# Gate chunks before a branch projection, later transposes, split first loads, and identity products at the start of a hybrid decoder layer

## The chip, the cores and the metric

The kernel runs on one core of a Trainium2 chip. The metric is the device time of one execution, in microseconds (us), as the median of the runs shown. A profiled execution gives the trace; its span runs from the first to the last instruction. Engines are named as in the profile: PE (TensorE, matrix products) with PEld (its weight loads), DVE (VectorE), ACT (ScalarE), POOL (GpSimd) and SP (SyncE, which here only issues DMAs).

## The reference, cut to what matters

One decoder layer with 256 tokens and 2048 channels, all in float32:

```
h  = rms_norm(x, norm_mix)
qa,ka,va, u, qc,kc,vc, gates = split(h @ w_in)       # 3*1024, 1024, 3*1024, 3*2048 columns
ya = block_attention(qa,ka,va)                       # "a": softmax with a relative bias
yb = multiscale_pool(u)                              # "b"
yc = stick_breaking_attention(qc,kc,vc)              # "c"
g  = sigmoid(gates)                                  # three gates of 2048 channels
m  = g[0]*(ya @ w_br_a) + g[1]*(yb @ w_br_b) + g[2]*(yc @ w_br_c)
x1 = x + m @ w_out
x2 = x1 + swiglu(rms_norm(x1, norm_ffn))             # 5632 hidden channels
out = rms_norm(x2, norm_final)
```

## The kernel before, in words

**Products.** Every float32 operand of a large product is split into two parts, hi (rounded) and lo (the rest), and a product is three: hi by hi, lo by hi, hi by lo. `split` (L105 to L112) does it: ACT writes hi (L108, with a scale L111), DVE subtracts to get lo (L109, L112). Splitting a piece of a weight matrix is called cutting it here. Output columns are worked in chunks of 512 (CH), rows of a weight matrix in units.

**Groups and units.** The work is a list of groups (L1008 to L1022), each one chunk of output columns, and each group is a list of units. A unit is fetched (DMA by SP), cut (ACT, DVE) and multiplied (PE). A projection of 2048 rows with two row tiles a unit has 8 units; `br`, a branch projection of 1024 rows, has 4 units for branch a (span 2) and 2 units for b and c (span 4). `gate(n, 0, ...)` has 8 units. `gate_pair` works two chunks at once by a form of Strassen's scheme (class `Squares`): seven PSUM banks collect the partial products, and its units come in three kinds, N (24 products), Wp (9) and Ws (12), in the order N Wp Ws N Wp Ws N Wp Ws Wp Ws N.

**Order.** `run` (L475) goes through the units. Before unit j is multiplied, the units up to j+3 are cut (two ahead in the first six units), as far as a bound on slots allows; `ahead` issues the fetches. DVE, ACT, PE and SP each execute their own instructions in the order in which they are written out, so a unit's cut stands behind all that was written out earlier on DVE and ACT. In the first eight units, the cut is preceded by `prepare_x`, which transposes two column tiles of x on PE and splits them; that of unit 1 is written out before unit 0 is multiplied.

**Work beside.** `beside(gen, after, lag)` puts a generator on a list; `step_side` advances one generator after each unit: the first on the list that is due, `after` units after it was put there, then every `lag` units. The end of a generator takes a step of its own. An advanced generator goes to the end of the list. `finish_side` (L269) advances until the list is empty, with no units between.

- Stick-breaking attention (branch c): `all_stick`, four pairs of heads; each pair takes five units of steps: scores (L667, L669) and exponentials (L674 to L677); sums (L679, L680) and masks; split; a step left out, then triangular products (L689 to L691) and exponentials (L692); values (L583, L584) with the next pair's scores. It starts two units after the last group of qkv c.
- `br(0, 0)` calls `finish_side` ahead of its first unit, then `open_late`, which replaces a pool of buffers, and then puts `add_differences` on the list (eight steps, every second unit), whose results `gate_pair` needs.
- The merged sums m, after branch c: `turn()` of `br(n, 2)` transposes 4 tiles of 128 columns in two steps. `transposed` (L234) takes a PSUM bank, two transposes on PE (L238), hi on ACT, lo on DVE; the bank is free when lo is written. For n = 0 and 1 these steps fall into the following `gate_pair(1, 2)`.

**Buffers.** `slots` has 22 tiles of 8 KB a partition for weights, x and intermediate results; `wk` has 8 tiles of 128 by 512; PSUM has 8 banks.

**Start and end.** SP issues mix_rows, both x tiles (128 tokens by 512 columns each), and the first weights as four parts of 256 KB, then further x columns and weights. PE's first instruction is `columns(0, mix_rows)`. At the end each half of the tokens is normalised, scaled by DVE (n = 0, 3) and ACT (n = 1, 2), and written by four DMAs on SP (L1000 to L1006). The first half's writing goes on while PE works on the second half.

The order of the groups around the change:

```
groups += qkv("c", 4 * WIDTH, start_stick)
groups += [gate(n, 0, True) for n in range(2)] + [br(n, 0, True) for n in range(2)]
for n in range(2, D_MODEL // CH):
    groups += [gate(n, 0, False), br(n, 0)]
```

With the third argument True, `gate` writes its scaled sums without the sigmoid, and `br` applies it (L845), so that ACT keeps the tables of the exponentials while stick attention runs.

Of the kernel before, what the change touches and what calls it, by code (L numbers as in the profile page):

```python
# [16 lines left out]
P = 128  # L17
D_MODEL = 2048
SEQ = 256
# [13 lines left out]
CH = 512  # L33
# [18 lines left out]
def trunk(ctx: ExitStack, tc: tile.TileContext, x, norm_mix, norm_ffn, w_in, w_pool, pool_scale,  # L52
# [49 lines left out]
    def toks(t):  # L102
        return slice(t * P, (t + 1) * P)
# [85 lines left out]
    def load_x(c):  # L189
        for t in range(NT):  # L190
            nc.sync.dma_start(xt[t][:, cols(c)], x[toks(t), cols(c)])

    mix_rows = const.tile([KT, P], F32, name="mix_rows")
    nc.sync.dma_start(mix_rows, norm_mix[0].rearrange("(k p) -> k p", p=P))
    load_x(0)
    nrows = const.tile([KT + HEADS, P], F32, name="nrows")
    rel = const.tile([HEADS, REL_BUCKETS], F32, name="rel")

# [4 lines left out]
    def columns(c, rows):  # L203
        k = rows.shape[0]
        pt = bank()
        nc.tensor.transpose(pt[:, :k], rows, ident[:k, :k])
        nc.vector.tensor_copy(ncols[:, c:c + k], pt[:, :k])

    columns(0, mix_rows)

    def load_rows():
# [35 lines left out]
    def prepare_x(kt):  # L247
        transposed(xT(kt), [xt[t][:, kt * P:(kt + 1) * P] for t in range(NT)], ncols[:, kt:kt + 1])
# [5 lines left out]
    def beside(gen, after=2, lag=2):  # L254
        side.append([clock[0] + after, lag, gen])
# [219 lines left out]
    def run(units, startup):  # L475
        loads = [u for _, u in units if u.loads]
        done = {"fetch": 0, "cut": 0}

        def fetch():
            k = done["fetch"]  # L480
            if k in (1, 2, 3):
                load_x(k)
            if k == 4:
                load_rows()
            if k == 0:
                loads[k].fetch(parts=4)
            else:
                loads[k].fetch()
            done["fetch"] += 1

        def ahead(n):
            while done["fetch"] < min(n, len(loads)):
                fetch()

        opened = 0
        j = 0
        while j < len(units):
            lead = 2 if j < KT // 2 - 2 else 4
            if j == 0:
                ahead(2)  # L500
            while done["cut"] < min(j + lead, len(units)):
                u = done["cut"]
                g, unit = units[u]
                if u >= KT // 2 and sum(v.need for _, v in units[j:u]) + unit.need > cap[0]:
                    break
                if j:
                    ahead(opened + 3 if u > 7 else opened + 2)
                if u < KT // 2:
                    prepare_x(2 * u)
                    prepare_x(2 * u + 1)  # L510
                    unit.cut(step=None if u else 1)
                else:
                    unit.cut()
                done["cut"] += 1
                opened = sum(v.loads for _, v in units[:u + 2]) - 1 if u + 1 < len(units) else opened + 1
            if j:
                ahead(opened + 3 if done["cut"] > 7 else opened + 2)
            g, unit = units[j]
            if unit.first and g.before:
                g.before()  # L520
            if g.staggered and len(units) - j == 2:
                for p in range(len(g.parts)):
                    for k in range(2):
                        units[j + k][1].multiply([p])
                    g.after(g.acc[p], *g.parts[p])
                return
            unit.multiply()
            if j in startup:
                startup[j]()
            if unit.last:  # L530
                g.after(g.acc if isinstance(g, Group) else g.banks)
            clock[0] += 1
            step_side()
            j += 1
# [282 lines left out]
    def br(n, b, plain=False):  # L817
# [21 lines left out]
        def after(acc):  # L839
            if b == 2 and n == 0:  # L840
                mT.append(Halves())
            for t in range(NT):
                g = gates[n][t]
                if plain:
                    nc.scalar.activation(g, g, AF.Sigmoid)  # L845
                if b == 0:
                    nc.vector.tensor_mul(m[n][t], acc[t], g)
                else:
                    nc.vector.tensor_mul(g, acc[t], g)
                    nc.vector.tensor_add(m[n][t], m[n][t], g)  # L850
            if b == 2:
                beside(turn(), lag=1)

        return Group(lhs, range(HEADS), w_br[b], 0, n * CH, after, before, span=4 if b else 2)

# [128 lines left out]
    def final_norm(acc, t, c):  # L984
# [15 lines left out]
        for n in (0, 1, 3, 2):  # L1000
            hn = h[t][:, cols(n)]
            if n in (0, 3):
                nc.vector.tensor_scalar(hn, hn, a[9], None, OP.mult)
            else:
                nc.scalar.activation(hn, hn, AF.Copy, scale=a[9])
            nc.sync.dma_start(out[toks(t), cols(n)], hn)  # L1006

    groups = qkv("a", 0, start_block)  # L1008
    groups += [channels("u", 3 * WIDTH, c, start_pooling if c else None) for c in range(2)]
    groups += qkv("c", 4 * WIDTH, start_stick)  # L1010
    groups += [gate(n, 0, True) for n in range(2)] + [br(n, 0, True) for n in range(2)]
    for n in range(2, D_MODEL // CH):
        groups += [gate(n, 0, False), br(n, 0)]
    for b in range(1, 3):
        for i in range(2):
            groups += [gate_pair(i, b), br(2 * i, b), br(2 * i + 1, b)]
# [48 lines left out]
```

## Time and profile before

| | us |
|---|---|
| median of 3 runs | 1577.0 (1576.76 to 1577.03) |
| the profiled execution | 1576.42 |
| its span | 1574.7 |
| PE busy | 1545.7 (98%) |
| DVE busy | 1094.3 (69%) |
| ACT busy | 745.9 (47%) |
| mean granted clock of PE, share of full speed | 0.994 |

The first table of the profile gives the busy time of each engine. A line of the trace in time order gives the start, the length, the engine, the line of the program and the operation, what is written from what, and in brackets how long the engine sat idle before and what ended that. A row of merged instructions (x4) gives their common length. PE's products overlap: one starts before the one ahead of it has ended, so the step from start to start is its cost.

### The profile page before, as it was taken

The numbers are of one execution on the slowest core, as the hardware profiler recorded it, in microseconds if no ns is written. First come the engines' busy times: TensorE is split into PE (matmuls) and PEld (weight loads), VectorE is DVE, ScalarE is ACT, GpSimd is POOL, SyncE is SP. The second block draws the span as 40 slices with busy tenths as digits, with TensorE's granted clock in tenths as the row PEclk, the third lists the DMA queues.
The fourth block names the chain that finished last, engine by engine and source line by source line (L and its number), as shares of the span: only waits on it lengthen the run. The fifth ranks groups of instructions, "written<-read, shape, count | busy, mean of one in ns | idle before, by whom it ended". The sixth has DMA issues, their size and how long they took to land.

```text
span 1574.7 us, 19128 instructions
## 1 busy us (share of the span) xinstructions
PE 1545.7 (98%) x7873; PEld 1322.6 (84%) x7873; DVE 1094.3 (69%) x1064; ACT 745.9 (47%) x724; POOL 25.6 (2%) x94
## 2 busy tenths in 40 slices
PE   8999999999799999999999999999999999999997
PEld 8998999988688888877888878888888888888886
DVE  6453665644486988978556888667886668867685
ACT  7423443446454545635455555434454435543363
POOL 2000000101000000000000000000000000000000
PEclk9999999999899999999999999999999999999999
DMA  9654455553355745647555655556665556655661
GB/s 344 219 188 161 142 186 174 168 187 134 116 179 200 249 151 205 242 148 257 188 190 174 214 187 204 197 162 212 212 213 190 165 185 212 226 191 172 208 219 54
DMA packets 144167, 300.12 MB, mean 191 GB/s; under 512 B 6432, under 2 KB 7504, under 8 KB 143952
## 3 DMA queue, kind: packets, MB, share of 16 engines
q1 hardware_dynamic: 143776, 297.84, 55.7%
q8 instruction: 61, 1.00, 0.3%
q0 software_dynamic: 304, 1.06, 0.2%
q14 instruction: 26, 0.21, 0.0%
HBM read 296.77 MB, written 2.11 MB: 190 GB/s over the span
## 4 chain that ended last, share of the span: by engine, by line
PE 96%; DVE 2%; ACT 1%; issue 0%; DMA 0%; POOL 0%; SPq 0%; ACTq 0%; DVEq 0%; POOLq 0%
PE bank L440 37%; PE bank L333 13%; PE bank L334 13%; PE bank L338 13%; PE bank L353 5%; PE bank L355 5%; PE bank L361 5%; DVE slot L109 1%; PE bank L938 1%; ACT slot L108 1%; PE bank L583 1%; PE bank L238 0%; DMA slot<-in_x_dram 0%; PE bank L584 0%; DVE slot L422 0%
## 5 line engine op out<-in xcount | busy, mean ns | idle before, releaser
L109 DVE TENSOR_TENSOR slot<-slot,slot 128x2048 fp32r<-128x2048 f32 (+3 forms) x406 | 719.3, 1799 | 191.0 <-ACT slot L108 190.0
L108 ACT ACTIVATE slot<-slot 128x2048 fp32r<-128x2048 f32 (+3 forms) x406 | 601.5, 1517 | 346.6 <-DVE slot L424 136.8
L440 PE MATMUL bank<-slot,slot 128*128 128x512 f32 x1719 | 440.4, 391 | 0.0
L440 PEld LDWEIGHTS bank<-slot,slot 128*128 128x128 f32 x1719 | 322.7, 188 | 66.8
L333 PE MATMUL bank<-slot,slot 128*128 128x512 f32 (+1 forms) x936 | 365.0, 390 | 0.0
L334 PE MATMUL bank<-slot,slot 128*128 128x512 f32 (+1 forms) x936 | 362.8, 388 | 0.0
L440 PE MATMUL bank<-slot,late 128*128 128x512 f32 x1014 | 279.1, 390 | 0.0
L338 PE MATMUL bank<-slot,slot 128*128 128x512 f32 (+1 forms) x936 | 236.5, 387 | 0.0
L440 PEld LDWEIGHTS bank<-slot,late 128*128 128x128 f32 x1014 | 189.7, 188 | 39.2 <-DVE slot L109 0.2
L333 PEld LDWEIGHTS bank<-slot,slot 128*128 128x128 f32 x936 | 176.4, 188 | 35.4
L334 PEld LDWEIGHTS bank<-slot,slot 128*128 128x128 f32 x936 | 176.3, 188 | 35.3
L338 PEld LDWEIGHTS bank<-slot,slot 128*128 128x128 f32 x936 | 174.9, 188 | 35.9
L353 PE MATMUL bank<-slot,slot 128*128 128x256 f32 x640 | 159.6, 287 | 0.2 <-ACT slot L108 0.2
L355 PE MATMUL bank<-slot,slot 128*128 128x256 f32 x640 | 157.7, 284 | 0.0
L353 PEld LDWEIGHTS bank<-slot,slot 128*128 128x128 f32 x640 | 123.5, 193 | 0.7 <-ACT slot L108 0.6
L355 PEld LDWEIGHTS bank<-slot,slot 128*128 128x128 f32 x640 | 123.5, 193 | 0.0
L361 PE MATMUL bank<-slot,slot 128*128 128x256 f32 x640 | 89.8, 283 | 0.0
L108 ACT ACTIVATE slot<-bank 128x512 fp32r<-128x512 f32 (+1 forms) x46 | 23.2, 520 | 127.6 <-PE bank L938 67.7
L361 PEld LDWEIGHTS bank<-slot,slot 128*128 128x128 f32 x640 | 82.6, 192 | 0.0
L109 DVE TENSOR_TENSOR slot<-bank,slot 128x512 fp32r<-128x512 f32 (+1 forms) x46 | 26.8, 596 | 56.6 <-ACT slot L108 56.6
L422 DVE TENSOR_TENSOR slot<-slot 128x1024 f32<-128x1024 f32 x49 | 59.7, 1219 | 0.0
L973 DVE TENSOR_TENSOR slot<-bank,slot 128x512 f32<-128x512 f32 x30 | 19.6, 686 | 55.5 <-PE bank L338 55.5
(158 smaller groups left out, 626.1 us busy)
## 6 DMA issues: line engine op xcount, KB each, us to landing
slot<-in_w_in_dram SPq DMA_DIRECT2D x103, 1024.0 KB, 5.0
slot<-in_w_gate_dram SPq DMA_DIRECT2D x88, 512.0 KB, 3.9
slot<-in_w_up_dram SPq DMA_DIRECT2D x88, 512.0 KB, 4.9
slot<-in_w_down_dram SPq DMA_DIRECT2D x44, 1024.0 KB, 5.2
slot<-in_w_out_dram SPq DMA_DIRECT2D x16, 1024.0 KB, 5.6
slot<-in_w_br_a_dram SPq DMA_DIRECT2D x8, 1024.0 KB, 5.1
slot<-in_w_br_b_dram SPq DMA_DIRECT2D x8, 1024.0 KB, 5.4
slot<-in_w_br_c_dram SPq DMA_DIRECT2D x8, 1024.0 KB, 5.1
```

What stands on the lines that cost most here:

```text
L108: nc.scalar.activation(hi, src, AF.Copy)
L109: nc.vector.tensor_tensor(lo, src, f32(hi), OP.subtract)
L333: nc.tensor.matmul(acc[:, c], hi[:, toks(t)], whi[:, j, c], start=i + j == 0, stop=False)
L334: nc.tensor.matmul(acc[:, c], lo[:, toks(t)], whi[:, j, c], start=False, stop=False)
L338: nc.tensor.matmul(acc[:, c], hi[:, toks(t)], wlo[:, j, c], start=False, stop=i + j == n - 1)
L353: nc.tensor.matmul(o, whi[:, j, w], hi, start=i + j == 0 and c % 2 == 0, stop=False, skip_group_check=True)
L355: nc.tensor.matmul(o, whi[:, j, w], lo, start=False, stop=False, skip_group_check=True)
L361: nc.tensor.matmul(o, wlo[:, j, w], hi, start=False, stop=i + j == n - 1 and c % 2 == 1, skip_group_check=True)
L422: nc.vector.tensor_tensor(s[:, 0:2], raw[:, 0:1].to_broadcast([P, 2, CH]), raw[:, 1:3], OP.add)
L440: nc.tensor.matmul(g.banks[b], x, w[:, k, :], start=start, stop=g.left[b] == 0)
L583: nc.tensor.matmul(py[:, i, :], v[:, 0, s], pA[i], start=True, stop=False)
L973: nc.vector.tensor_add(h[t][:, cs], acc[t], h[t][:, cs])
```

## The change

- Group order: gate chunks 0, 1, 2, then `br` 0, 1, 2 of branch a (all with the sigmoid in `br`), then gate chunk 3 and `br` 3. Before it was gate 0, 1, br 0, 1, gate 2, br 2, gate 3, br 3.
- `turn()` of `br(0, 2)` and `br(1, 2)` becomes due 4 units after it is listed, not 2.
- The first x load is split: columns 0 to 255 of tokens 0 to 127 on SP, those of tokens 128 to 255 on ACT's queue, then mix_rows and columns 256 to 511 of both on ACT's queue. mix_rows and `load_x(0)` leave SP.
- `warm_up(n)` multiplies the identity by itself n times into a PSUM bank that nothing reads: 8 times ahead of `columns(0, ...)`, and 3 times after the transposes of unit 0.
- In the final writing, the DMAs of n = 1 and 2 are issued by ACT.

```diff
@@ -191,8 +191,12 @@
     mix_rows = const.tile([KT, P], F32, name="mix_rows")
-    nc.sync.dma_start(mix_rows, norm_mix[0].rearrange("(k p) -> k p", p=P))
-    load_x(0)
+    first, rest = slice(0, SEQ), slice(SEQ, CH)
+    nc.sync.dma_start(xt[0][:, first], x[toks(0), first])
+    nc.scalar.dma_start(xt[1][:, first], x[toks(1), first])
+    nc.scalar.dma_start(mix_rows, norm_mix[0].rearrange("(k p) -> k p", p=P))
+    for t in range(NT):
+        nc.scalar.dma_start(xt[t][:, rest], x[toks(t), rest])
@@ -206,6 +210,13 @@
+    def warm_up(n):
+
+        o = bank()
+        for _ in range(n):
+            nc.tensor.matmul(o[:, :P], ident, ident, start=True, stop=True)
+
+    warm_up(8)
     columns(0, mix_rows)
@@ -508,6 +519,8 @@
                     prepare_x(2 * u)
                     prepare_x(2 * u + 1)
+                    if u == 0:
+                        warm_up(3)
                     unit.cut(step=None if u else 1)
@@ -849,7 +862,7 @@
             if b == 2:
-                beside(turn(), lag=1)
+                beside(turn(), after=4 if n < 2 else 2, lag=1)
@@ -1003,14 +1016,13 @@
-            nc.sync.dma_start(out[toks(t), cols(n)], hn)
+            (nc.sync if n in (0, 3) else nc.scalar).dma_start(out[toks(t), cols(n)], hn)
-    groups += [gate(n, 0, True) for n in range(2)] + [br(n, 0, True) for n in range(2)]
-    for n in range(2, D_MODEL // CH):
-        groups += [gate(n, 0, False), br(n, 0)]
+    groups += [gate(n, 0, True) for n in range(3)] + [br(n, 0, True) for n in range(3)]
+    groups += [gate(3, 0, False), br(3, 0)]
```

## Rows read from the trace of the kernel before

**Rows 1.** The page's first table: busy time of each engine, its share of the span, and its instructions.

```profile
PE 1545.7 (98%) x7873; PEld 1322.6 (84%) x7873; DVE 1094.3 (69%) x1064; ACT 745.9 (47%) x724; POOL 25.6 (2%) x94
```

**Rows 2.** PE's waits over the whole span: what waited for what, us in total, how often, the longest.

```profile
PE bank L689 <- ACT t L108: 7.1, 1, 7.1
PE bank L238 <- DVE slot L109: 5.2, 1, 5.2
PE bank L238 <- DMA slot<-in_x_dram: 3.4, 2, 2.3
```

**Rows 3.** Busy time in stretches of 20 us: the stretch, its length, then PE, PEld, DVE, ACT and POOL with their instructions, the granted clock of PE as a share of full speed, the DMA share and GB/s.

```profile
400.00:420.00 20.00, 11.99 (x47) 9.83 (x46) 5.73 (x7) 10.26 (x17) 2.30 (x6) 0.76 0.32 106
...
700.00:720.00 20.00, 14.79 (x66) 11.93 (x65) 14.42 (x16) 9.20 (x11) 0.00 (x0) 0.91 0.32 106
```

**Rows 4.** PE in order of time, from the triangular products of the third pair of heads to the values of the fourth.

```profile
398.78 0.39 PE L689 MATMUL bank<-t,tri 128*128 128x512 f32 x1
...
399.71 0.40 PE L333 MATMUL bank<-slot,slot 128*128 128x512 f32 x1
...
402.46 0.59 PE L583 MATMUL bank<-t,slot 128*128 128x256 f32 x2
...
403.76 0.60 PE L667 MATMUL bank<-slot,slot 128*128 128x256 f32 x2
...
404.85 0.38 PE L669 MATMUL bank<-slot,slot 128*128 128x128 f32 x2
412.30 0.79 PE L689 MATMUL bank<-t,tri 128*128 128x512 f32 x1 [7.07 <-ACT t L108]
...
415.46 1.22 PE L583 MATMUL bank<-t,slot 128*128 128x256 f32 x2 [0.95 <-POOL t L656]
416.48 0.63 PE L584 MATMUL bank<-t,slot 128*128 128x128 f32 x2
```

**Rows 5.** PE in order of time, the first unit of `br(0, 0)`: its first product, and the four products that end it.

```profile
418.04 0.77 PE L333 MATMUL bank<-slot,slot 128*128 128x512 f32 x1
...
421.13 1.07 PE L338 MATMUL bank<-slot,slot 128*128 128x512 f32 x4
```

**Rows 6.** DVE in order of time: the gated products after `br(1, 0)`, then the first instruction (L174) of three successive steps of `add_differences`; between these stand the rest of the step and the lo parts of two cuts.

```profile
442.09 1.28 DVE L847 TENSOR_TENSOR slot<-bank,wk 128x512 f32<-128x512 f32 x2
443.29 0.69 DVE L174 TENSOR_TENSOR wk<-slot 128x512 f32<-128x512 f32 x1
...
448.14 0.69 DVE L174 TENSOR_TENSOR wk<-slot 128x512 f32<-128x512 f32 x1
...
453.86 0.69 DVE L174 TENSOR_TENSOR wk<-slot 128x512 f32<-128x512 f32 x1
```

**Rows 7.** All engines in order of time at the begin of `gate_pair(1, 2)`: every row of PE that transposes m for n = 0 and 1 (L238), and the rows of DVE and PE around the wait.

```profile
694.05 0.60 PE L238 MATMUL bank<-ident,slot 128*128 128x128 f32 x4
...
699.99 0.60 PE L238 MATMUL bank<-ident,slot 128*128 128x128 f32 x4
...
702.49 0.60 PE L238 MATMUL bank<-ident,slot 128*128 128x128 f32 x4
...
704.00 1.22 DVE L422 TENSOR_TENSOR slot<-slot 128x1024 f32<-128x1024 f32 x1
...
705.74 0.38 PE L238 MATMUL bank<-ident,slot 128*128 128x128 f32 x2
...
710.85 0.42 DVE L109 TENSOR_TENSOR slot<-bank,slot 128x256 fp32r<-128x256 f32 x1
...
711.33 0.69 PE L238 MATMUL bank<-ident,slot 128*128 128x128 f32 x2 [5.21 <-DVE slot L109]
...
711.66 4.13 PE L440 MATMUL bank<-slot,slot 128*128 128x512 f32 x12
...
712.47 0.43 DVE L109 TENSOR_TENSOR slot<-bank,slot 128x256 fp32r<-128x256 f32 x1 [1.20 <-ACT slot L108]
```

**Rows 8.** All engines in order of time at the start: PE's transposes of x for units 0 and 1, the first and the last products of unit 0, and the transposes for unit 2.

```profile
6.63 1.76 PE L238 MATMUL bank<-ident,slot 128*128 128x128 f32 x7 [1.17 <-DMA slot<-in_x_dram]
...
8.62 0.58 PE L353 MATMUL bank<-slot,slot 128*128 128x256 f32 x1 [0.23 <-ACT slot L108]
...
11.66 1.12 PE L361 MATMUL bank<-slot,slot 128*128 128x256 f32 x8
...
12.62 0.60 PE L238 MATMUL bank<-ident,slot 128*128 128x128 f32 x4
```

**Rows 9.** The chain that ended last, in order of time, at the start: start, length, what.

```profile
1.72 4.87 DMA slot<-in_x_dram
```

**Rows 10.** All engines in order of time at the end: the scaling of the first half of the tokens and what follows it on ACT and DVE, and the last four issues of the output on SP.

```profile
1563.48 1.34 ACT L1005 ACTIVATE slot<-slot,st 128x512 f32<-128x512 f32 x2 [1.21 <-DVE st L999]
...
1564.73 0.42 ACT L989 ACTIVATE wk<-slot 128x256 f32<-128x256 f32 x1
...
1566.24 0.42 DVE L988 TENSOR_TENSOR slot<-bank,slot 128x256 f32<-128x256 f32 x1 [0.47 <-PE bank L338]
...
1569.05 1.80 SPq L1006 DMA_DIRECT2D out_dram<-slot  x4
```

**Rows 11.** DMA issues of two short stretches (2.1 to 2.6 us, the first part of the first weights; 4.05 to 5.1 us, the second x columns): what is loaded, how often, KB each, us from issue to landing.

```profile
slot<-in_w_in_dram SPq DMA_DIRECT2D x1, 256.0 KB, 5.1
...
slot<-in_x_dram SPq DMA_DIRECT2D x2, 256.0 KB, 6.0
```

## The prediction

> **What bounds the kernel now.** I read the table of busy times first: PE is busy 98% of the span, DVE 69%, ACT 47% [rows 1]. So only what lets PE idle, or slows its clock, can give time back, and what DVE and ACT do more counts only where PE comes to wait for it. Next the list of PE's waits [rows 2]. Three stand out: 7.1 us once for the hi part of a stick-attention tile, 5.2 us once for a transpose (L238) that waits for a DVE instruction, and 3.4 us for the first x loads. The table of stretches then shows what a wait costs beside itself: around 400 us PE is busy 12.0 of 20 us and its mean granted clock is 0.76, around 700 us 14.8 of 20 us and 0.91 [rows 3]; elsewhere the lower of its two levels (1.2 and 2.4 GHz) hardly shows. The reader is to see that four places are in play (start, 405, 705 and the end) and that each long wait is followed by some microseconds at half clock. The lines in order of time at those places price the parts.
>
> **Part 1, three gate chunks ahead of branch a.** Stick attention starts two units after qkv c, takes five units for a pair of heads and four pairs, so its last step falls in the 22nd unit. Before, two gate chunks give 16 units; the rest of the fourth pair is worked off in `finish_side` with no units between, and PE waits there. With three chunks there are 24 units, so the list is empty when `br(0, 0)` begins. What that is worth: PE's last score products start at 404.85, so the next could start near 405.05; the first product of `br(0, 0)` starts at 418.04. Between lie products that take 0.93 us (398.78 to 399.71) and 1.30 us (402.46 to 403.76) when the same step of the third pair stands among units [rows 4, 5]. Lost: 418.04 - 405.05 - 2.23 = 10.8 us. After it the first eight products take 3.09 us (418.04 to 421.13); the four that follow start (1.07 - 0.40)/3 = 0.22 us apart, so eight cost 1.8 at full clock: 1.3 us more [rows 4, 5]. Sum **-12.1**. The cover is the eight units of gate chunk 2, some 22 us; the wait list has the triangular products waiting once only, so those of the three pairs that stood among units were hidden [rows 2].
>
> What becomes late next: three branch groups in a row, with `add_differences` beside them. DVE needs 4.85 us for a step of kind N with two cuts (443.29 to 448.14), 5.72 for one of kind W (448.14 to 453.86), and 1.28 for the gated products after each group [rows 6]. Twelve units of 12 products at 0.22 to 0.23 are 32.5 us of PE; six steps (three of each kind) and three sets of gated products are 31.7 + 3.8 = 35.5 us of DVE. It falls 3 us behind, but cuts are written out three units (8 us) ahead, and eight gate units follow with little else on DVE. I take 0, with 0 to +3 as bounds. The gate sums that now wait in six of the eight `wk` tiles leave two for a step, which is what one step uses.
>
> **Part 2, transposes of m later.** Count units from the end of `br(1, 2)`, and call the first unit of `gate_pair(1, 2)` u0. Before, the four steps stand after `br(1, 2)`, u0, u1 and u2, at 694.05, 699.99, 702.49 and 705.74 [rows 7]. Each transposes two tiles, and each tile needs a PSUM bank. After u2 (N, Wp and Ws done) seven banks hold partial products and one is left. So the second tile of that step waits until the first one's lo part is written, and DVE does that at 710.85, behind the sums and lo parts of two cuts that it began at 704.00: this is the wait of 5.21 us [rows 7]. Now the change. With `after=4` the first chunk's steps fall after u0 and u1. The second chunk's first step falls after u2, a generator's end takes the turn after u3, and its second step falls after u4. **A step after u2 is still there**, behind the same cuts and with one free bank, so I expect the 5.2 us to stay. The step after u4 is new, with one free bank as well; no cut is written out between u3's and it, so DVE is free, and the second tile waits only for the first one's hi and lo: from the begin of a transpose to the end of lo took 711.33 to 712.90, 1.6 us, here at the lower clock; less its own 0.3, some 1.2 us [rows 7]. The step that leaves 694.05 had no wait. Sum **+1.2**; below, 0; above, +6.5, if the new step meets DVE as busy as the old one (5.2 and the slow products after it).
>
> **Part 3, the start.** PE's transposes of x now go on at 6.63, when the second x load has landed (4.87 us after 1.72); unit 0's first product starts at 8.62, after hi parts and the first cut [rows 8, 9]. Unit 0's first 16 products take 3.04 us (8.62 to 11.66); its last eight take 1.12 together, 0.12 apart, so 16 cost 1.9 at full clock [rows 8]. *The clock:* 11 identity products (two instructions each) keep PE at work beforehand. A pair of instructions with 256 columns took 1.02 us at the lower clock (415.46 to 416.48), so one with 128 some 0.5, and eight some 4 us [rows 4]. Begun when the identity is written, near 2 us (an estimate), they end near 6, before x is complete, so they cost nothing and I count the 1.1 us in full (0 if the clock doesn't rise). *The loads:* unit 1's transposes are written out ahead of unit 0's products and need columns 256 to 511, so the last x load decides again. It is now the fourth issue on ACT, and issues cost 1.80/4 = 0.45 us each [rows 10], so it goes out about as late as now, but unit 0's hi parts and first cut no longer stand behind it: what follows is four transposes, 0.6 us [rows 8], in place of 2.0. The first weights go out two issues earlier, 0.9 us, and took 5.1 us [rows 11]: they land near 6.4, and the cut adds 0.6. So the first product starts between 7.0 and 7.8; I take 7.5, **-1.1**. The next cover is thin: the second x columns, issued near 4.1 and 4.6, take 6.0 us and are needed for the transposes at 12.62 [rows 8, 11]; with 0.9 us earlier issue they land at 9.2 to 9.7, for a need near 10.4. Both together **-2.2**, bounds 0 and -3.2. ACT's four issues take 1.8 us, ahead of its table load and constants, all before its first hi part near 6.
>
> Here a rule speaks against the change. The row says that the second x load, 256 KB, took 4.87 us after its issue [rows 9]. The Trainium skill ("DMA: Bandwidth & Descriptors", section "Issuing engines are not separate DMA queues") says that all queues end on the same 16 DMA engines, so that a second one saves only the time of issuing. By that the loads give one issue, 0.45, in place of 1.1, and the total would be 0.6 us higher.
>
> **Part 4, the end.** ACT scales two chunks in 1.34 us [rows 10]. If an issue holds ACT as it holds SP, 0.45 us each, the two of the first half push the square at 1564.73 back by 0.9; DVE had 0.47 us of idle before 1566.24 [rows 10], so the last chain starts 0.4 later. At the very end SP's four issues take 1.80 us after DVE's first scaling, which is half of that pair's time; ACT's two scalings and two issues in turn take 0.67 + 0.45 + 0.67 + 0.45 = 2.2, the same end. Sum **+0.4**. If an issue costs ACT nothing, the last one goes out some 0.5 us earlier: -0.5. No row shows an issue on ACT; I take the upper end, since SP's rows are the nearest.
>
> The Trainium skill ("Perfetto Trace Analysis", section "DMA Instruction — HWDGE (DVE, Sync)") says that the issuing sequencer is free only when the descriptors are generated. By that the end costs the 0.4; without it the total would be 0.9 lower.
>
> **Sum.** -12.1 + 1.2 - 2.2 + 0.4 = -12.7 on the profiled execution's 1576.4, so 1563.7; the median is 0.6 above that execution: 1564.3 us.
>
> **Rivals.** (a) *The wait at 705 goes too.* For it: a bank or DVE could be free earlier with the first step moved from 694 on. Against: the three steps after u0, u1, u2 keep their places. Then 5.2, the slow products after it (12 take 4.13 against 12 x 0.225 = 2.7, so 1.3 [rows 7]) and the new 1.2 are gained: 1556.6. Chance 0.16. (b) *DVE falls behind in the branch groups*, or the new step after u4 meets a busy DVE: +3 to +5, 1567 to 1569. For it: the 35.5 against 32.5 us above. Chance 0.13. (c) *Slower than before:* the steps of `add_differences` come into PE's way whole, because slots or `wk` tiles shorten the lead of the cuts to nothing. A step is 2.4 (N) or 3.3 us (W) of DVE without its cuts of 2.4 [rows 6]; six of them are 17 us, so 1581. It decides from 2.1 us of PE wait a step (12.7/6) on. Against it: the lead of three units, and no such wait in the list with the same steps [rows 2]. Chance 0.03. (d) *The change doesn't do what it says:* the list isn't empty at `br(0, 0)`, and the wait stays: 1564.3 + 12.1 = 1576. Chance 0.04.
>
> **How the numbers follow.** The forecast has 0.64, with 1561 to 1566.5 from the bounds of parts 3 and 4. Range 1556 to 1568: it takes in (a) and most of (b). About 0.2%, 3 us, is what a measurement can tell from no change. Faster: 0.64 + 0.16 + 0.13 = 0.93; same: (d), 0.04; slower: (c), 0.03.
>
> **What the trace after would show.** Part 1: no PE wait at L689, clock at full before `br(0, 0)`, ACT's L845 after the third gate chunk. Part 2: an L238 wait of some 5 us after the third unit of `gate_pair(1, 2)`, and one near 1 us two units later; (a) is right if the first is missing. Part 3: first L353 near 7.5, 0.12 us apart at once. Part 4: ACT's square after the first half's scaling some 0.9 later than the scaling's end. A PE wait for L109 or L108 in `br(1, 0)` or `br(2, 0)` would speak for (b) or (c). The forecast is wrong above all if the bank count of part 2 is.

## The result and the profile after

| | before | after |
|---|---|---|
| median, us (4 runs each) | 1576.88 (1576.66 to 1577.03) | 1565.60 (1565.12 to 1565.91) |
| ratio, 95% interval | | 0.9928 [0.9911, 0.9945] |
| the profiled execution, us | 1576.42 | 1565.91 |
| its span, us | 1574.7 | 1564.1 |
| granted clock of PE, mean | 0.994 | 0.996 |

The change takes 11.3 us off; 1564.3 was predicted, with 1556 to 1568 as range. Line numbers after the change are some 11 to 14 higher: the transposes L238 are now L249, the triangular products L702, the products of `Squares` L451, the first product L364, the output L1018 and L1019.

The first table of the page after and PE's list of waits (what waited for what, us in total, times, longest), to lay beside [rows 1, 2]:

```profile
PE 1545.4 (99%) x7895; PEld 1322.9 (85%) x7895; DVE 1093.8 (70%) x1064; ACT 746.3 (48%) x726; POOL 25.9 (2%) x94
```

```profile
PE bank L249 <- DVE slot L109: 6.1, 2, 5.2
...
PE bank L249 <- DMA slot<-in_x_dram: 0.6, 1, 0.6
```

The 7.1 us at the triangular products are gone, the 5.2 us at the transposes are not: that wait now comes twice, 5.2 and 0.9. PE is busy as long as before (1545.4 against 1545.7), with 22 identity instructions more; the span lost idle time, and fewer products run at the lower clock.

Part 1 in the table of stretches (columns as in [rows 3]) and in PE's order of time, where the fourth pair's triangular products now stand among units:

```profile
400.00:420.00 20.00, 20.00 (x98) 16.98 (x97) 9.74 (x11) 11.58 (x17) 2.51 (x4) 1.00 0.55 189
440.00:460.00 20.00, 20.00 (x90) 16.55 (x89) 15.74 (x25) 10.22 (x14) 0.00 (x0) 1.00 0.50 168
```

```profile
413.22 1.07 PE L349 MATMUL bank<-slot,slot 128*128 128x512 f32 x4
414.12 0.39 PE L702 MATMUL bank<-t,tri 128*128 128x512 f32 x1
```

From 400 to 420 PE was busy 12.0 of 20 us at a clock of 0.76 [rows 3]; now it is 20.0 of 20 at 1.00. The triangular products start 0.9 us after the four products ahead of them, and the row notes no idle time. In the second stretch, where branch groups and the steps of `add_differences` run, DVE works 15.7 of 20 us and PE still never waits.

Part 2, PE at the begin of `gate_pair(1, 2)` (the transposing step after u0, the one after u2, the one after u4), and under it DVE around the two waits, with ACT's hi part of the first tile:

```profile
685.74 0.60 PE L249 MATMUL bank<-ident,slot 128*128 128x128 f32 x4
...
691.53 0.38 PE L249 MATMUL bank<-ident,slot 128*128 128x128 f32 x2
697.09 0.69 PE L249 MATMUL bank<-ident,slot 128*128 128x128 f32 x2 [5.18 <-DVE slot L109]
697.43 5.09 PE L451 MATMUL bank<-slot,slot 128*128 128x512 f32 x12
702.36 1.09 PE L451 MATMUL bank<-slot,late 128*128 128x512 f32 x4
...
707.14 0.38 PE L249 MATMUL bank<-ident,slot 128*128 128x128 f32 x2
708.46 0.44 PE L249 MATMUL bank<-ident,slot 128*128 128x128 f32 x2 [0.93 <-DVE slot L109]
708.65 1.63 PE L451 MATMUL bank<-slot,late 128*128 128x512 f32 x6
```

```profile
694.28 0.37 ACT L108 ACTIVATE slot<-bank 128x256 fp32r<-128x256 f32 x1
694.41 2.29 DVE L109 TENSOR_TENSOR slot<-slot,slot 128x2048 fp32r<-128x2048 f32 x1 [0.31 <-ACT slot L108]
696.62 0.41 DVE L109 TENSOR_TENSOR slot<-bank,slot 128x256 fp32r<-128x256 f32 x1
...
707.98 0.42 DVE L109 TENSOR_TENSOR slot<-bank,slot 128x256 fp32r<-128x256 f32 x1 [5.66 <-ACT slot L108]
```

The lo part that frees the bank after u2 starts when a cut of 2.29 us has ended, without a gap: it was queued. So was the hi part that it needs: the tile's transposes began at 691.53, ACT wrote the hi part from 694.28 on, without a gap behind a cut of its own. That cut had itself waited 1.75 us for sums on DVE. So of the 5.18 us some 2.7 pass before the lo part could start at all (694.28 + 0.37), and the rest behind the cut. The one after u4 follows 5.66 us of idle DVE: there only the chain of transpose, hi and lo is waited for.

Part 3, PE at the start, with the DMA on the chain of waits at the same place (start, length, what):

```profile
1.43 3.78 PE L217 MATMUL bank<-ident 128*128 128x128 f32 x16 [1.43 <-POOL ident masks.py:199]
...
7.51 0.55 PE L249 MATMUL bank<-ident,slot 128*128 128x128 f32 x3 [0.61 <-DMA slot<-in_x_dram]
7.81 0.36 PE L364 MATMUL bank<-slot,slot 128*128 128x256 f32 x1
...
9.81 1.12 PE L372 MATMUL bank<-slot,slot 128*128 128x256 f32 x8
```

```profile
2.20 5.26 DMA slot<-in_x_dram
```

The first product starts at 7.81 (before 8.62 [rows 8]) and the first sixteen take 2.00 us (7.81 to 9.81) in place of 3.04.

Part 4, ACT at the end: scaling and issue in turn for the first half, then the first square of the second half, then the final scaling.

```profile
1552.01 0.72 ACT L1018 ACTIVATE slot<-slot,st 128x512 f32<-128x512 f32 x1 [1.21 <-DVE st L1012]
1552.77 0.35 ACTq L1019 DMA_DIRECT2D out_dram<-slot  x1
1553.16 0.72 ACT L1018 ACTIVATE slot<-slot,st 128x512 f32<-128x512 f32 x1 [0.43 <-ACT slot L1018]
...
1554.31 0.42 ACT L1002 ACTIVATE wk<-slot 128x256 f32<-128x256 f32 x1 [0.43 <-ACT slot L1018]
...
1557.55 0.72 ACT L1018 ACTIVATE slot<-slot,st 128x512 f32<-128x512 f32 x1 [0.94 <-DVE st L1012]
```

The square comes 2.30 us after the first scaling's start, before 1.25 [rows 10].

**Where the 10.6 us between the two spans lie.** The same instruction is looked up in both traces, and the distance between its two times is followed along the span. At the last products of unit 0: 11.66 - 9.81 = 1.85 us. At the step after u0: 699.99 - 685.74 = 14.25, of which 0.35 is the step at 694.05, which no longer stands ahead of it; so part 1 gave 14.25 - 1.85 - 0.35 = 12.05. At the end of the slow products after the 5.2 us wait (715.63 in the row below): 715.63 - 702.36 = 13.27, since the same twelve products took 3.97 us before and 4.93 after. The step after u4, which the kernel before doesn't have, takes 1.51 us (707.14 to 708.65), which leaves 11.76. At the first scaling of the end it is 1563.48 - 1552.01 = 11.47; the 0.29 between, over 840 us, I can't place. From there to the end of the span before takes 11.22 us and after 12.09: 11.47 - 0.87 = 10.6.

The kernel before, PE's row behind the slow products and ACT's final scaling, neither shown so far:

```profile
715.63 0.62 PE L440 MATMUL bank<-slot,late 128*128 128x512 f32 x2
```

```profile
1568.54 1.33 ACT L1005 ACTIVATE slot<-slot,st 128x512 f32<-128x512 f32 x2 [0.94 <-DVE st L999]
```

### The profile page after: what moved, and what is told of

It reads as the page before. It is cut to its first block, busy times and chain, and to the rows that moved or that the text cites. A ratio compares the mean times of both kernels' runs of the same rounds, so it can differ in the third digit from the quotient of the medians.

```text
span 1564.1 us, 19170 instructions
## 1 busy us (share of the span) xinstructions
PE 1545.4 (99%) x7895; PEld 1322.9 (85%) x7895; DVE 1093.8 (70%) x1064; ACT 746.3 (48%) x726; POOL 25.9 (2%) x94
## 4 chain that ended last, share of the span: by engine, by line
PE 96%; DVE 2%; ACT 1%; issue 0%; DMA 0%; ACTq 0%; DVEq 0%
PE bank L451 38%; PE bank L344 13%; PE bank L345 13%; PE bank L349 13%; PE bank L364 5%; PE bank L372 5%; PE bank L366 5%; DVE slot L109 1%; PE bank L951 1%; ACT slot L108 1%; PE bank L249 0%; PE bank L596 0%; DMA slot<-in_x_dram 0%; PE bank L597 0%; DVE slot L433 0%
## 5 line engine op out<-in xcount | busy, mean ns | idle before, releaser
L109 DVE TENSOR_TENSOR slot<-slot,slot 128x2048 fp32r<-128x2048 f32 (+3 forms) x406 | 719.0, 1798 | 187.3 <-ACT slot L108 186.8
L108 ACT ACTIVATE slot<-slot 128x2048 fp32r<-128x2048 f32 (+3 forms) x406 | 600.8, 1516 | 339.8 <-DVE slot L435 135.9
L451 PE MATMUL bank<-slot,slot 128*128 128x512 f32 x1719 | 441.3, 391 | 0.0
L451 PEld LDWEIGHTS bank<-slot,slot 128*128 128x128 f32 x1719 | 323.4, 189 | 67.0
L451 PE MATMUL bank<-slot,late 128*128 128x512 f32 x1014 | 279.4, 390 | 0.0
L451 PEld LDWEIGHTS bank<-slot,late 128*128 128x128 f32 x1014 | 189.6, 188 | 39.3 <-DVE slot L109 0.2
L364 PE MATMUL bank<-slot,slot 128*128 128x256 f32 x640 | 158.6, 286 | 0.0
L364 PEld LDWEIGHTS bank<-slot,slot 128*128 128x128 f32 x640 | 122.7, 192 | 0.1
L108 ACT ACTIVATE slot<-bank 128x512 fp32r<-128x512 f32 (+1 forms) x46 | 23.3, 520 | 132.0 <-PE bank L951 67.8
L109 DVE TENSOR_TENSOR slot<-bank,slot 128x512 fp32r<-128x512 f32 (+1 forms) x46 | 26.9, 595 | 59.4 <-ACT slot L108 59.4
```

What stands on the lines that cost most here:

```text
L108: nc.scalar.activation(hi, src, AF.Copy)
L109: nc.vector.tensor_tensor(lo, src, f32(hi), OP.subtract)
L364: nc.tensor.matmul(o, whi[:, j, w], hi, start=i + j == 0 and c % 2 == 0, stop=False, skip_group_check=True)
L451: nc.tensor.matmul(g.banks[b], x, w[:, k, :], start=start, stop=g.left[b] == 0)
```

## The experiments

Each was timed beside the kernel before on the same chip, and a ratio is always to that: 1577.48 us for e1 to e4, 1577.52 for e5 to e8, 1577.60 for e9 to e11, 1577.72 for e12, against 1576.88 in the table above. So a median can be compared with the whole change's 1565.60 only to within some 0.8 us. The first four put one part alone into the kernel before; the theory is the prediction's four terms.

**e1_order: the order of the groups alone.**

```diff
-    groups += [gate(n, 0, True) for n in range(2)] + [br(n, 0, True) for n in range(2)]
-    for n in range(2, D_MODEL // CH):
-        groups += [gate(n, 0, False), br(n, 0)]
+    groups += [gate(n, 0, True) for n in range(3)] + [br(n, 0, True) for n in range(3)]
+    groups += [gate(3, 0, False), br(3, 0)]
```

> The kernel before with the new group order alone. Theory (the parts add up; the order is worth the wait in finish_side and the slow products after it): 1576.9 - 11.9 = 1565.0 us, no PE wait at the triangular products, no other new wait. Rival (the order alone is worth the whole change or more, because the later transposes or the end lose what it gains; or less, because the wait moves to the branch groups): below 1564 or above 1567.

1565.86 us against 1577.48: -11.6, ratio 0.9927 [0.9915, 0.994]. The triangular products are off the list of waits; the long wait at 705 stands as before, now at 700 (PE in order of time):

```profile
699.73 0.69 PE L238 MATMUL bank<-ident,slot 128*128 128x128 f32 x2 [5.21 <-DVE slot L109]
700.07 5.05 PE L440 MATMUL bank<-slot,slot 128*128 128x512 f32 x12
704.96 1.08 PE L440 MATMUL bank<-slot,late 128*128 128x512 f32 x4
```

So the order alone makes practically the whole gain, and no wait of PE took the place of the old one.

**e2_turn: the later transposes alone.**

```diff
-                beside(turn(), lag=1)
+                beside(turn(), after=4 if n < 2 else 2, lag=1)
```

> The kernel before with the later transposes alone (after=4 for n below 2). Theory (a step still falls after the third unit with one bank free, and a new one two units later): the wait of 5.2 us stays and one near 1 us is added, 1576.9 + 1.5 to 2.1 = 1578.4 to 1579.0 us. Rival (the later turn takes the wait away): 1570 us.

1578.36, ratio 1.0006 [0.9996, 1.0015]: +0.9 (1.5 to 2.1 was expected), not to be told from none by the time alone. The rows tell it: the old wait stays and a second one is new, as after the whole change.

```profile
711.63 0.62 PE L238 MATMUL bank<-ident,slot 128*128 128x128 f32 x2 [5.18 <-DVE slot L109]
...
722.32 0.44 PE L238 MATMUL bank<-ident,slot 128*128 128x128 f32 x2 [0.93 <-DVE slot L109]
```

**e3_start: the loads and the identity products alone.**

```diff
-    nc.sync.dma_start(mix_rows, norm_mix[0].rearrange("(k p) -> k p", p=P))
-    load_x(0)
+    first, rest = slice(0, SEQ), slice(SEQ, CH)
+    nc.sync.dma_start(xt[0][:, first], x[toks(0), first])
+    nc.scalar.dma_start(xt[1][:, first], x[toks(1), first])
+    nc.scalar.dma_start(mix_rows, norm_mix[0].rearrange("(k p) -> k p", p=P))
+    for t in range(NT):
+        nc.scalar.dma_start(xt[t][:, rest], x[toks(t), rest])
...
+    warm_up(8)
     columns(0, mix_rows)
...
                     prepare_x(2 * u + 1)
+                    if u == 0:
+                        warm_up(3)
```

> The kernel before with the new loads and the identity products alone. Theory: the first products start 0.8 us earlier and run at full clock, 1576.9 - 1.9 = 1575.0 us. Rival (DMA or ACT eats it within the first 40 us): 1576.9 us.

1575.88, ratio 0.9991 [0.9982, 1.0]: -1.6, at the edge of what the time alone can tell. The first product starts at 7.79 and the last eight of unit 0 at 9.79, as in the whole change. But the end is later: from the final scaling to the end of the span (1573.7) it takes 1573.7 - 1567.15 = 6.55 us, against 1574.7 - 1568.54 = 6.16 before, though the output goes by SP as before.

```profile
1567.15 1.33 ACT L1018 ACTIVATE slot<-slot,st 128x512 f32<-128x512 f32 x2 [0.94 <-DVE st L1012]
```

**e4_end: the output issues on ACT alone.**

```diff
-            nc.sync.dma_start(out[toks(t), cols(n)], hn)
+            (nc.sync if n in (0, 3) else nc.scalar).dma_start(out[toks(t), cols(n)], hn)
```

> The kernel before with the output of n = 1 and 2 issued by ACT alone. Theory (an issue holds ACT, so the second half's square and then the last scaling and issue come later): 1576.9 + 0.9 = 1577.8 us. Rival (two queues shorten the end): 1576.4 us.

1578.16, ratio 1.0003 [0.9995, 1.0012]: +0.7, not to be told from none by the time alone. From the first scaling to the final one it takes 1570.39 - 1564.82 = 5.57 us, against 5.06 before; from there to the end of the span (1576.6) 6.21, as before.

```profile
1564.82 0.72 ACT L1005 ACTIVATE slot<-slot,st 128x512 f32<-128x512 f32 x1 [1.21 <-DVE st L999]
...
1570.39 0.72 ACT L1005 ACTIVATE slot<-slot,st 128x512 f32<-128x512 f32 x1 [0.94 <-DVE st L999]
```

So the 0.87 us at the end of the whole change are two things: 0.5 from the issues on ACT, and 0.4 that come with the new start. All traces agree on the second: from the final scaling to the end of the span it is 6.14 to 6.21 us in the four with the old loads (the kernel before, e1, e2, e4) and 6.50 to 6.62 in the ten with x split, in either order of the pieces. e6 below, which has the new loads without the identity products, is among the ten with 6.60, so the loads make it and not these products. The 0.4 lie behind the output itself: in all fourteen traces the DMA stops moving bytes 4.55 to 4.73 us after the final scaling begins (read in slices of 0.175 us). The four singles sum to -11.6 + 0.9 - 1.6 + 0.7 = -11.6, the whole change gives -11.3: within what these medians can tell, the parts add up.

**e5_onebank: the whole change, with a step's two tiles in the halves of one PSUM bank.** Theory: one free bank makes the 5.2 us; rival: DVE's cuts make it, whatever the banks.

```diff
-            for j in range(4):
-                transposed(mT[0](4 * n + j), [m[n][t][:, j * P:(j + 1) * P] for t in range(NT)])
-                if j % 2:
-                    yield
+            for i in range(2):
+                pt = bank()
+                for j in range(2):
+                    for t in range(NT):
+                        c = 2 * i + j
+                        nc.tensor.transpose(pt[:, j * SEQ + t * P:j * SEQ + (t + 1) * P], m[n][t][:, c * P:(c + 1) * P], ident)
+                split(*mT[0].pair(2 * n + i), pair(pt))
+                yield
```

> The changed kernel, with the two tiles of a turn step in the two halves of one PSUM bank (one split of 512 columns in place of two of 256); the steps keep their places. Theory (the second tile waits for a bank): no PE wait at these transposes, neither the 5.2 us nor the 0.9 us, and no slow products after it: 1565.7 - 5.2 - 2.2 - 0.9 = 1557.4 us. Rival (DVE is behind there, and PE meets it at the next cut instead): 1563 to 1565.7 us, with the wait moved to the products of gate_pair.

1556.95, ratio 0.9871 [0.9858, 0.9885]: 8.6 less than the whole change by the two medians, 9.3 with each taken against the kernel before beside it (-20.6 and -11.3). No transpose of m waits any more, and the twelve products after u2 take 2.85 us (691.88 to 694.73):

```profile
691.52 0.60 PE L852 MATMUL bank<-ident,slot 128*128 128x128 f32 x4
691.88 3.01 PE L451 MATMUL bank<-slot,slot 128*128 128x512 f32 x12
694.73 1.07 PE L451 MATMUL bank<-slot,late 128*128 128x512 f32 x4
```

```profile
697.06 0.69 DVE L109 TENSOR_TENSOR slot<-bank,slot 128x512 fp32r<-128x512 f32 x1
```

The second fence is the lo part of that step on DVE. It comes 5.5 us after the transposes (5.1 in the whole change), so the queues of ACT and DVE are no shorter; PE only has no second tile to place in the meantime.

The step after u2 costs 0.36 instead of 5.90, the slow products 2.85 instead of 4.93, the step after u4 0.35 instead of 1.51: 8.8 us by the rows.

**e7_spare: the bank count tested in another way.** Each tile keeps its own bank; the steps are moved to places where more banks are free: due after 2 units again, and neither `turn` nor the generator of the gates ahead of it takes a step for its end.

```diff
                 gates[2 * i + n] = [c[t][n] for t in range(NT)]
+            return
             yield
...
-                if j % 2:
+                if j == 1:
                     yield
...
-                beside(turn(), after=4 if n < 2 else 2, lag=1)
+                beside(turn(), lag=1)
```

> The changed kernel, with two banks a step as before, but turn due after 2 units again and the generators of turn and of gate_pair's end without a step of their own for their ends, so that all four steps fall ahead of the third unit of gate_pair(1, 2), when at least three banks are free. Theory (banks): 1557.4 us, as in the run with one bank. Rival (DVE is behind after the transposes wherever they stand): a wait of some us stays, 1563 us or more.

1557.42, ratio 0.9874 [0.9859, 0.9889]. The steps stand at 675.24, 681.17, 687.08 and 689.59, each four transposes of 0.60 us, and the product behind each follows 0.35 or 0.36 us later, with no wait; the last of them:

```profile
689.59 0.60 PE L249 MATMUL bank<-ident,slot 128*128 128x128 f32 x4
689.95 1.70 PE L451 MATMUL bank<-slot,late 128*128 128x512 f32 x6
```

Fewer banks needed (e5), or more of them free (e7): both take the wait away. In e5 the step stands behind the same cuts as in the whole change; in e7 it stands ahead of them, so e7 by itself would leave open whether the bank or the cuts count; e5 settles that.

**e6_nowarm: the whole change without the identity products.**

```diff
-    warm_up(8)
     columns(0, mix_rows)
...
-                    if u == 0:
-                        warm_up(3)
```

> The changed kernel without the identity products, with the new loads. Theory (they raise the clock of the first unit): its first products start within 0.3 us of 7.8 and are 0.21 us apart at first, 1565.7 + 1.1 = 1566.8 us. Rival (the clock would be up by then anyway, or the products delay the transposes as much as they give): 1565.7 us.

1567.28, ratio 0.9937 [0.9925, 0.995]: 1.7 more than the whole change by the two medians, 1.0 with each against the kernel before beside it, so the rows are to tell. The first product starts at 8.00; PE's products of unit 0 are 0.21 us apart until 10.06, and 0.12 after that. The transposes for unit 2 start at 11.88, with the identity products at 10.77: 1.11 us, of which 0.19 in the start of the first product (8.00 against 7.81) and 0.92 in the first sixteen (2.92 against 2.00).

```profile
8.57 0.41 PE L357 MATMUL bank<-slot,slot 128*128 128x256 f32 x1
8.78 0.41 PE L359 MATMUL bank<-slot,slot 128*128 128x256 f32 x1
...
10.92 1.12 PE L365 MATMUL bank<-slot,slot 128*128 128x256 f32 x8
11.88 0.60 PE L242 MATMUL bank<-ident,slot 128*128 128x128 f32 x4
```

**e8_best and e10_sp_end: one bank, and all output on SP**, with the transposes as early as before the change (e8, `beside(turn(), lag=1)`) or as late as after it (e10). The edit of e5 is in both; the third:

```diff
-            (nc.sync if n in (0, 3) else nc.scalar).dma_start(out[toks(t), cols(n)], hn)
+            nc.sync.dma_start(out[toks(t), cols(n)], hn)
```

> The changed kernel with one bank a step, turn due after 2 units as before, and all output issued by SP. If the parts add: 1557.4 - 0.7 = 1556.7 us. Rival (with the wait gone, something else near it comes to bind): 1559 us or more.

> The version with both tiles of a transposing step in one bank and the later transposes kept, but all output DMAs on SP as before the change. Against it the earlier version with one bank measured 1556.95. Theory (an issue on ACT delays the last half by about 0.4 to 0.9 us): 1556.2 to 1556.5, first scaling to the end 11.6 us instead of 12.1. Rival (the output queue doesn't matter at this level): 1556.95. Beside it the version with the early transposes as well measured 1556.93; if this one measures 1556.3, the early timing costs 0.5; if 1556.9, neither matters.

1556.93 (ratio 0.9871 [0.9857, 0.9884]) and 1556.97 (0.9868 [0.9855, 0.9882]). Neither is faster than e5 by the median. In the traces the end did become shorter, from first scaling to the end of the span 1555.2 - 1543.60 = 11.60 in e10 against 1555.2 - 1543.07 = 12.13 in e5; but in e10's execution the last products of unit 0 started at 10.26 (in e8's at 10.27), in e5's at 9.66, with the same code there. The start differs between executions by as much as the end gains. With one bank the timing of the transposes makes no difference.

**e9_rest: the rest pieces of x ahead of the norm rows**, one on each queue; the rest is the whole change.

```diff
+    nc.sync.dma_start(xt[0][:, rest], x[toks(0), rest])
+    nc.scalar.dma_start(xt[1][:, rest], x[toks(1), rest])
     nc.scalar.dma_start(mix_rows, norm_mix[0].rearrange("(k p) -> k p", p=P))
-    for t in range(NT):
-        nc.scalar.dma_start(xt[t][:, rest], x[toks(t), rest])
```

> The changed kernel, but the two rest pieces of x (columns 256 to 511) are issued ahead of the norm rows, one on SP and one on ACT, each directly behind its first piece. In the trace of the changed kernel the last rest piece was issued at about 2.20 us and landed 5.26 us later, and PE waited for it 0.61 us. Theory (the landing time is set by the place in the issue order): issued some 0.9 us earlier it lands near 6.6, no wait for x, first product 0.4 to 0.7 us earlier, near 7.2, 1565.1. The norm rows come one issue (0.45 us) later, so columns at 5.6 instead of 5.14; that is no later than the rest needs. Rival (the transfers share engines with the weights, so that the landing doesn't come earlier, or the norm rows decide now): first product at 7.8 or later, 1565.6 to 1566.0.

1565.66, ratio 0.9926 [0.9913, 0.9938]: no gain that the time can tell. Yet x did come earlier, and PE waits for it no more. The last rest piece of the whole change (issued at 2.20) and e9's rest piece on SP (issued at 1.25), as what, engine, how often, KB, us from issue to landing; the landing of e9's other piece isn't in the profile:

```profile
slot<-in_x_dram ACTq DMA_DIRECT2D x1, 128.0 KB, 5.3
```

```profile
slot<-in_x_dram SPq DMA_DIRECT2D x1, 128.0 KB, 3.2
```

PE in e9, with no gap from 5.25 on:

```profile
5.25 0.28 PE L210 MATMUL bank<-ident,mix_rows 16*128 16x16 f32 x1
...
6.37 1.22 PE L217 MATMUL bank<-ident 128*128 128x128 f32 x6
7.43 0.60 PE L249 MATMUL bank<-ident,slot 128*128 128x128 f32 x4
7.78 0.36 PE L364 MATMUL bank<-slot,slot 128*128 128x256 f32 x1
```

The first product stands at 7.78 as before. The theory failed in its result: what x no longer delays, the identity products and the first transposes do, which fill PE up to 7.43. e3, whose start is that of the whole change, shows the same: no wait for x, the last transposes at 7.37, the first product at 7.79.

**e11_all: one bank, early transposes, all output on SP, and these loads.**

Its edits are those of e8 and e9 together.

> One bank for a transposing step, transposes as early as before the change, all output on SP, and the rest pieces of x ahead of the norm rows. If the pieces are additive: 1556.4 (1556.93 less 0.5 for the start). If the start doesn't gain: 1556.9.

1557.4, ratio 0.9874 [0.9859, 0.9889]: not faster than the other three versions with one bank.

**e12_fewer: e11 with 6 + 1 identity products instead of 8 + 3.**

```diff
-    warm_up(8)
+    warm_up(6)
...
-                        warm_up(3)
+                        warm_up(1)
```

> The version with one bank, early transposes, all output on SP and the rest pieces of x first, with fewer identity products: 6 ahead of the norm rows instead of 8, and 1 after the first transposes instead of 3. In that version the identity products filled 1.43 to 5.21 and 6.37 to 7.4 without a gap, and the first product started at 7.66. Theory (with x there in time, the identity products are what the first product waits for): two products fewer at 0.47 us each let the norm rows' transpose start near 4.65, when the rows land, and the first transposes 0.6 us earlier; the second block 0.7 shorter; first product between 7.0 and 7.2, and still 0.12 us apart. Rival (the clock needs the whole block): the first 16 products take 3.0 us instead of 2.0, and the next transposes start as late as with the full block, near 10.6 or later. In time: theory 0.5 less than 1557.4, rival the same; by the median alone this is hardly to be told, the rows are to decide.

1557.62, ratio 0.9872 [0.9856, 0.9889]. The rows decide for the rival: the first product starts at 7.88, later than 7.66, and the first sixteen take 3.08 us (7.88 to 10.96).

```profile
5.46 0.28 PE L210 MATMUL bank<-ident,mix_rows 16*128 16x16 f32 x1 [1.10 <-DMA mix_rows<-in_norm_mix_dram]
...
7.88 0.58 PE L364 MATMUL bank<-slot,slot 128*128 128x256 f32 x1
...
10.96 1.13 PE L372 MATMUL bank<-slot,slot 128*128 128x256 f32 x8
```

The norm rows landed at 5.42, not near 4.65, so the shorter first block only opened a gap of 1.10 us, and with the gap and fewer products the clock was still low at the first product. Which of the two kept it low, this run doesn't separate.

## Why the prediction was right, step by step

**Part 1** was sized right: -12.1 predicted, -12.05 in the trace, -11.6 by the medians of e1. The doubt about DVE in three branch groups (0 to +3, rival b) came to nothing: no wait of `br` for L109 or L108 stands in the list. Rival (d) fell, since no wait at L702 is left, and rival (c), since PE is busy throughout the stretch at 440; the other half of rival (b), a busy DVE at the step after u4, fell with the 5.66 us that DVE is idle there.

**Part 2** held in its mechanism and its size. The forecast that a step after u2 is still there, with one free bank, and that the 5.2 us stay, was the point that separated it from rival (a); the row shows 5.18, and e5 and e7 show that with a bank to spare it is gone. How long it lasts is set by the queues in front of the tile's hi part on ACT and lo part on DVE; the prediction named DVE alone. The new step cost 1.51 - 0.35 = +1.16, forecast +1.2, but the wait is 0.93 where 1.2 was estimated at the lower clock, and the other 0.23 is the step's own transposes, now cut in two; so that the sum agrees to 0.04 is luck in part. In the two profiled executions part 2 looks 0.96 worse, because the products after the same wait took 4.93 instead of 3.97 us. That isn't the change: of the eight traces with this wait, the four with the old transposes have 3.97, 4.89 (e1: 700.07 to 704.96, above), 4.99 (e3) and 5.27 (e4), the four with the later ones 4.93, 4.35 (e2), 4.92 (e6) and 4.07 (e9: 697.40 to 701.47).

```profile
697.40 4.23 PE L451 MATMUL bank<-slot,slot 128*128 128x512 f32 x12
701.47 1.07 PE L451 MATMUL bank<-slot,late 128*128 128x512 f32 x4
```

The profiled execution of before was one with a short slow stretch, so comparing the two traces charges the change with 0.96 us that isn't its own.

**Part 3** is one of the two mis-sized terms: -2.2 predicted, -1.85 at the start of the trace, and 0.4 of that given back at the end of the span. The clock gave 1.04 in the first sixteen products (3.04 to 2.00); without the identity products e6 loses 1.11, as forecast (1.1). The loads gave 0.81, forecast 1.1: the last piece of x was issued at 2.20, not "about as late as now" (1.72), and took 5.26 us for 128 KB, where 4.87 for 256 KB had been the row; what follows it took 0.30 instead of 0.6. The rule of the Trainium skill that was weighed here ("DMA: Bandwidth & Descriptors", section "Issuing engines are not separate DMA queues") gave 0.45 for the loads; the measured 0.81 lies between it and the forecast.

The first product came at 7.81, 0.01 outside the interval 7.0 to 7.8; with the same start it came at 7.67 in e5, 7.79 in e3, 8.20 in e7, 8.27 in e10 and 8.28 in e8, with the old one at 8.60 to 8.70 (the kernel before, e1, e2, e4). So the 0.81 is one draw from some 0.3 to 1.0, and that part 3 came this near its -2.2 is luck in part. That the identity products "cost nothing" held only while x was late: in e9, and with the change's own loads in e3, they and the transposes behind them fill PE without a wait until the last transposes, at 7.43 and 7.37.

The 0.4 at the end was not foreseen at all. It stands in e3, where ACT issues no output, and in e6, without the identity products, and not in e4, where ACT does issue output; what in the loads makes it stays open.

**Part 4** went as worked out where it was worked out: ACT is held by an issue (0.35 us, within the 0.43 that lie between the end of one ACT instruction and the start of the next), the square comes 1.05 later (2.30 instead of 1.25; forecast 0.9), and 0.5 of it reaches the final scaling (5.54 against 5.06 in the whole change, 5.57 in e4; forecast 0.4). "The same end" for the last pair held in e4 too (6.21 against 6.16). The section of the Trainium skill cited for it ("Perfetto Trace Analysis", "DMA Instruction — HWDGE (DVE, Sync)") agrees with these rows: ACT's next scaling starts at 1553.16, 0.04 after its issue has ended (1552.77 + 0.35).

**The sum**: -12.05 + 1.16 - 1.85 + 0.48 + 0.39 = -11.9 in the traces, with 0.96 for the length of the slow stretch and 0.29 unplaced -10.6; forecast -12.7. By the medians -11.3. Of the 1.3 us by which the forecast was too low, the start (0.35) and the end (0.47) are 0.8; the other 0.5 is less than the 1.3 us by which the slow products after one and the same wait differ between executions (3.97 to 5.27). One bound was put down wrongly: parts 3 and 4 alone give 1562.4 as the lower end of the forecast; its 1561 needs part 2's lower bound of 0 as well.

## What to carry to other kernels

Count, for each step that is worked off beside the main loop, in which unit it falls and how many PSUM banks are free there: moving the step left 5.2 us and the slow products after it where they were, and putting its two tiles into one bank took away 8.8 us by the rows. A long list of side work that runs out a few units before the point that empties it costs PE nothing; one chunk of other products ahead of that point was worth 11.6 us. An edit below 1 us is judged by the rows on which it acts, and in more than one execution where it can be, since starts of the same code lay 0.6 us apart.

## What the runs showed of the hardware beyond that

- The stretch at the lower clock after the same wait of 5.2 us, before the same twelve products, had no fixed length: they took 3.97, 4.07, 4.35, 4.89, 4.92, 4.93, 4.99 and 5.27 us in eight executions, 2.85 without the wait (e5).
- The smaller load on a second queue wasn't quicker: 5.12 to 5.73 us for the third piece of 128 KB on ACT's queue, beside the first weights, in the six traces where PE waits for it (the whole change, e5, e6, e7, e8, e10), against 4.85 to 4.95 us for 256 KB on SP's in four (the kernel before, e1, e2, e4).
- From the final scaling to the end of the span it took 6.50 to 6.62 us in the ten traces with the split x loads and 6.14 to 6.21 in the four without, though the output's bytes were moved in the same time in all fourteen; the cause is open.
